# Operands of a float32r matmul and their weights: another place within 128 bytes of SBUF

## The chip, the core and the metric

The kernel runs on one core of a Trainium2 chip. Its engines work side by side and wait for each other through semaphores: TensorE multiplies matrices (PE in the profile; its weight loads are listed apart, as PEld), VectorE (DVE), ScalarE (ACT) and GpSimd (POOL) work on elements, and SyncE (SP) issues the DMAs. On-chip memory, SBUF, has 128 partitions; a tile takes the same bytes of each partition, and "address" means here the byte within a partition. Matmuls write to PSUM.

The metric is the time on the device in microseconds (us), the median over several runs.

## The reference

One layer on 1024 tokens and 16 learned meta tokens, model width 1024, all in float32:

```
h = h + 0.5 * swiglu(rms_norm(h), gate1, up1, down1)      # FFN1, width 2816
proj = rms_norm(h) @ w_in
h = h + concat(stick_breaking_attention(proj), rwkv7_time_mix(proj)) @ w_out
h = h + 0.5 * swiglu(rms_norm(h), gate2, up2, down2)      # FFN2, width 2816
return rms_norm(h)[:, 16:]

swiglu(n, g, u, d) = (silu(n @ g) * (n @ u)) @ d
```

The attention has 8 heads of 64, the recurrence (RWKV-7) 8 heads of 64 with a state of 64 x 64 per head. Nearly all the arithmetic is in the matmuls with the big weight matrices.

## The kernel before

**Float32 in three products.** A float32 operand x is split into a high part `h` (x rounded to the format float32r by ScalarE) and a low part `l` (x minus `h`, by VectorE or GpSimd). A product of two such operands is three matmuls into the same PSUM tile (`mm3`): weights high by operand high, weights high by operand low, weights low by operand high. Weights come by DMA as `wraw` and are split into `whi` and `wlo`. Names that end in `h` and `l` are such pairs: `nh`, `nl` for the normalized input, `ah`, `al` for the activations between the FFN's matmuls.

In a matmul a block of 128 x 128 weights is stationary, and the other operand, 128 rows by up to 512 columns, moves past it. Each matmul has a weight load of its own, which runs beside the matmul before it.

**Two groups of tokens.** Group 0 has the meta tokens and the first 512 tokens (528 columns, `NA`), group 1 the other 512 (`NB`). The order is: FFN1 of group 0, projections of group 0, FFN1 of group 1, projections of group 1, w_out of group 0, FFN2 of group 0, w_out of group 1, FFN2 of group 1 (the "last FFN"); attention and recurrence are woven in between.

**Quads.** In FFN1 of group 0 and in the last FFN, the gate and up matmuls of most pairs of output blocks go another way. The two weight blocks of a pair (a1 and a2), the two halves of the inner dimension and the two halves of the columns form a 2 x 2 by 2 x 2 product, done with seven products in place of eight, as in Strassen's scheme (Winograd's form). `sums` makes the sums of operand halves: tiles `t1` to `t4`, each `h` and `l`, in `Fast.__init__`, of 4 inner blocks by w columns (w = 264 in FFN1, 256 in the last FFN). `pair` makes the sums of weight halves: GpSimd and VectorE write a sum to `qs`, ScalarE and VectorE split it into a pair of tiles `qh`, `ql` of 4 blocks by 128 columns. Two of the seven products use `whi` and `wlo` of a1 itself, the other five a `q` pair. `quad` runs the seven products in the order b11, b21, t1, t2, t4, b22, t3, where b11, b21 and b22 are parts of the normalized input (`n` in FFN1, `n2B` in the last FFN). One product is 4 inner blocks by 3 matmuls:

```
for k in range(4):
    mm(wh[:, k, :], xh[:, k], first and k == 0, False)
    mm(wh[:, k, :], xl[:, k], False, False)
    mm(wl[:, k, :], xh[:, k], False, k == 3)
```

So a pass of `quad` (one gate or up pair) is 7 x 12 = 84 matmuls: 24 with weights from `whi`/`wlo` and 60 with weights from `q`. FFN1 of group 0 has 8 gate and 7 up passes (output blocks 6 to 21, the last up pair goes the plain way), the last FFN 9 gate and 8 up passes (blocks 4 to 21). The order of gates, ups and downs is that of `quad_order`.

**Order of the work.** A planner (`Clock`) runs through the program when it is built: it prices each instruction by its engine and its shape, and issues in the order of its clock. It fixes the order of each engine's queue.

**Where tiles lie.** A pool is a stretch of SBUF in which its tiles stand one after another, each rounded up to 32 bytes. Pools are stacked from the left (from address 16512 up: `const`, `w`, `state`, `ffn`, `hn`, later `stage`) or from the right (from 229344 down). The pools of the quads are stacked from the right, in the order `p`, `t`, `q`; a pool `q` has 2 `wraw` of 4096 bytes, 7 `qh`, 7 `ql`, 3 `qs` and two pairs `ah`, `al`. A tile is written out in full rows, so that block k of a tile of [P, 4, w] begins 4 x w x k bytes after its start. The program before places what this change touches so:

| tile | pool, side | starts at | start modulo 128 | bytes from block to block |
|---|---|---|---|---|
| `ones` | `const`, left | 17024 | 0 | - |
| `whi`, `wlo` | `w`, left | 26816, 35008 and one 4096 on | 64 | 512 |
| `state0`, `state1` | `state`, left | 43200, 43712 | 64 | - |
| `ah`, `al` | `ffn`, left | 48320 and every 2112 on | 64 and 0 by turns | - |
| `nh0`, `nh1`, `nl0`, `nl1` | `hn`, left | 89856 and every 8448 on | 0 | 2112 |
| `t1h` and on, FFN1 | `t`, right | 176544 and every 4224 on | 32 | 1056 |
| `qh`, `ql`, FFN1 | `q`, right | 133280 and every 2048 on | 32 | 512 |
| `n2B` (`h0`, `h1`, `l0`, `l1`) | `f2b`, right | 196576 and every 8192 on | 96 | 2048 |
| `t1h` and on, last FFN | `t`, right | 128992 and every 4096 on | 96 | 1024 |
| `qh`, `ql`, last FFN | `q`, right | 85984 and every 2048 on | 96 | 512 |
| `ah`, `al`, last FFN's quads | `q`, right | 120800 and every 2048 on | 96 | - |
| `vs`, attention of group 0 | `attn0`, right | 179488, 184608 | 32 | 512 |
| `ath`, `atl`, attention of group 0 | `attn0`, right | 212960 and every 2048 on | 96 | - |

"Offset" below is the address at which the moving operand of a matmul starts, less the address at which the weights start that are loaded beside it, modulo 128. A moving operand of 256 columns is 1024 bytes of each partition, a block of weights 512.

Of the kernel before, what the change touches and what calls it, by code (L numbers as in the profile page):

```python
# [7 lines left out]
F32 = mybir.dt.float32  # L8
F32R = mybir.dt.float32r
# [7 lines left out]
P = 128  # L17
# [8 lines left out]
C = 64  # L26
# [13 lines left out]
        dict(raw=1, qs=4, kh=4, vs=2, sg=8, f=2, at=4, z=2, t=2, o=1)]  # L40
WOUT = ((0, 1, 2, 3, 4, 5, 6, 7, 2, 3, 4, 5), (0, 1, 2, 3, 4, 5, 6, 7))
QF = dict(ffn1=6, ffn2=4)
AHEAD = 0.1
IDLE = 0.45
BACKLOG = 3.0
# [14 lines left out]
def quad_order(nm):  # L60

    parts, qf = FPARTS[nm], QF[nm]
    for i, (f0, f1) in enumerate(parts):
# [26 lines left out]
class Eng:  # L90


    def __init__(self, real, name, clk):
        self._r, self._n, self._c = real, name, clk
# [94 lines left out]
class Clock:  # L189
# [195 lines left out]
    def catch_up(self, now):  # L385

        while True:
            best = nxt = None
            for e, l in self.pend.items():
                c, pick = self.clk[e], None  # L390
                for o in l:
                    t = o.at()
                    if t is None:
                        continue
                    key = (max(t, c, self.port if o.port else self.dma - BACKLOG if e == "s" else 0.0)
                           - AHEAD * (o.prio[0] == -self.URGENT), o.prio)
                    if pick is None or key < pick[0]:
# [67 lines left out]
class Fast:  # L465
# [3 lines left out]
    def __init__(self, pools, w):  # L469
        self.p, self.tp, self.q = pools  # L470
        self.w, self.nq, self.nc, self.ns, self.k = w, 7, 7, 4, 0
        self.t = {i: [self.tp.tile([P, 4, w], F32R, name="t%d%s" % (i, c)) for c in "hl"] for i in (1, 2, 3, 4)}


class Ker:
# [99 lines left out]
    def pair(self, raws, out):  # L575


        nc, p = self.nc, self.fast.q
        nb = self.fast.nq
        a1, a2 = raws  # L580
        lo4, hi4 = slice(0, 4), slice(4, 8)

        def part(src=None):

            for tag in ("qh", "ql"):
                yield self.need(bank=(p, tag, nb))
            if src:
                yield self.need(bank=(p, "qs", 3))
            self.clock.ahead = True
            t = [p.tile([P, 4, P], F32R, tag=tag, bufs=nb, name=tag) for tag in ("qh", "ql")]  # L590
            self.hold(t)
            if src:
                x, y, op, eng = src
                raw = p.tile([P, 4, P], F32, tag="qs", bufs=3, name="qs")
                self.hold((raw,))
                eng.tensor_tensor(out=raw, in0=x, in1=y, op=op)
                self.clock.ahead = False
                return t, raw
            return t

        def halves(t, raw):
            self.clock.ahead = True
            self.split(t[0], t[1], raw)
            self.clock.ahead = False
            self.drop((raw,))
            out.append((t, t))
        for tag in ("wh", "wl"):
            yield self.need(bank=(self.wp, tag, 2))
        self.clock.ahead = True
        w = [self.wp.tile([P, KT, P], F32R, tag="w" + c, bufs=2, name=n) for c, n in (("h", "whi"), ("l", "wlo"))]  # L610
        self.hold(w)
        self.clock.ahead = False
        s1 = yield from part((a2[:, lo4], a2[:, hi4], ALU.add, nc.gpsimd))
        self.clock.ahead = True
        self.split(w[0], w[1], a1)
        out.append(([w[0][:, lo4], w[1][:, lo4]], ()))
        out.append(([w[0][:, hi4], w[1][:, hi4]], w))
        self.clock.ahead = False
        s2 = yield from part((s1[1], a1[:, lo4], ALU.subtract, nc.vector))
        halves(*s1)  # L620
        a22 = yield from part()
        self.split(a22[0], a22[1], a2[:, hi4])
        self.clock.ahead = False
        s4 = yield from part((a1[:, hi4], s2[1], ALU.subtract, nc.vector))
        halves(*s2)
        out.append((a22, a22))
        s3 = yield from part((a1[:, lo4], a2[:, lo4], ALU.subtract, nc.gpsimd))
        halves(*s4)
        halves(*s3)
# [71 lines left out]
    def consts(self, cp):  # L701
        nc = self.nc
        self.ident = cp.tile([P, P], F32, name="ident")
        make_identity(self.tc.nc, self.ident)
        self.ones = cp.tile([P, P], F32, name="ones")
        nc.gpsimd.memset(self.ones, 1.0)

    def consts2(self, cp, xp, psp):
# [185 lines left out]
    def ffn(self, nm, h, n, chunks, edge, bank, first=None, hook=None, wx=False, poll=None, resid=None, done=None, wy=False, fast=False, once=False):  # L894
# [125 lines left out]
        act = []  # L1020
        qf, PS = (QF[nm], FPARTS[nm]) if fast else (0, PARTS)
        for part in PS:
# [250 lines left out]
    def plan(self):  # L1273
# [13 lines left out]
        def ffn(nm, poll=False, wx=False, fast=False, once=False):  # L1287
# [3 lines left out]
            def down(f0, f1, q):  # L1291
                dw = self.A[nm + "_w_down"][0].rearrange("(f p) m -> p f m", p=P)
                mw = KT // (f1 - f0) * P
                return dw[:, f0:f1, q * mw:q * mw + mw], f1 - f0, mw
            qf = QF.get(nm, 0)
            for f0, f1 in FPARTS[nm] if fast else PARTS:
# [800 lines left out]
    def pool(self, name, **k):  # L2097
        return Pool(self.tc.alloc_tile_pool(name=name, reuse_waits="tile", **k), self.clock)
# [6 lines left out]
    def body(self):  # L2105
        nc, A = self.nc, self.A
        pool = self.pool
        x, meta = A["x"][0], A["meta_tokens"]
        cp = pool("const", bufs=1)
# [10 lines left out]
        self.xbd = dt("xbd", [P, KT, NB])  # L2120


        self.sp = pool("state", bufs=1)
        self.fp = fp = pool("ffn", bufs=1)
        self.hp = pool("hn", bufs=1)
        h = self.hp.tile([P, KT, NA], F32, name="h")
# [6 lines left out]
        ext = [psp, "g", 4]  # L2133
# [153 lines left out]
        def firstA():  # L2287
            yield from self.ffn("ffn1", h, n, chA, chA, bank, first, hookA, True, None,
                                lambda: F.get("consts"), fast=True)
            ext.clear()  # L2290
            F["first"] = True
            self.carry = {k: self.stp.tile([P, 1], F32, name="car" + k)
                          for k in ["la", "lb"] + [a + str(i) for a in "rkv" for i in range(4)]}


        self.state = [self.sp.tile([P, 2, C], F32, name="state%d" % i) for i in range(2)]
        f2 = {}

        def task(gen, flag):
# [107 lines left out]
        def dense():  # L2407
            ch = [(0, 512)]
            yield from firstA()

            def load_n1(i):
# [85 lines left out]
        ck.spawn(self.loads(self.plan()), 41)  # L2497
        ck.spawn(self.splits(), 40)
        ck.run()
        for p_ in (ext[0], self.psd, f2["p"], fp, self.sp, self.wp, cp, self.dp):  # L2500
            p_.release()


# [28 lines left out]
```

## Time and profile before

| what | us |
|---|---|
| median of 3 runs | 2263.47 (2262.48 to 2263.78) |
| span of the profiled execution | 2259.5 |
| TensorE busy in it | 2232.4 |
| VectorE busy | 1550.5 |
| ScalarE busy | 1098.0 |
| GpSimd busy | 564.3 |
| matmuls, and weight loads | 16409 each |

The span runs from the first to the last instruction of one execution under the profiler. In the profile's rows a group reads: line, engine, operation, output tile <- input tiles, shape, xcount | busy us, mean ns of one | idle time before. All instructions have one line (L104), that of the helper which records them, so groups are told apart by tiles. Durations of matmuls overlap, since they are pipelined: what a matmul costs in a dense stretch is the distance from its start to the start of the next. That distance is read from the timeline, or from the chain of waits, whose merged pieces give the time and the number of matmuls in one stretch.

### The profile page before, as it was taken

How to read it: one execution, taken by the hardware profiler on the slowest of the kernel's cores; microseconds unless marked ns; L12 is line 12 of the kernel's file. 1: busy time of each engine (PE TensorE's matmuls, PEld its weight loads, DVE VectorE, ACT ScalarE, POOL GpSimd, SP SyncE). 2: the span in 40 equal slices, each digit the busy share in tenths (PEclk: the TensorE clock that was granted, in tenths of full speed). 3: DMA queues.
4: the chain of work that ended last, by engine and by line, in shares of the span. 5: the costliest groups of instructions: out<-in, count | busy, mean ns of one | idle time of the engine just before them, and what ended most of it. 6: DMA issues, size and time to landing. Idle time of an engine off the chain costs nothing.

```text
span 2259.5 us, 41724 instructions
## 1 busy us (share of the span) xinstructions
PE 2232.4 (99%) x16409; PEld 1978.1 (88%) x16409; DVE 1550.5 (69%) x2633; ACT 1098.0 (49%) x2176; POOL 564.3 (25%) x722
## 2 busy tenths in 40 slices
PE   9999999999999999999999999999999999999998
PEld 8999999999878888778778987887877899899998
DVE  5887776475666655576576787547777656897774
ACT  6444444534444434555435564445656335454444
POOL 1221111013143231532012324324443001221110
PEclk9999999999999999999999999999999999999999
DMA  5543332545633232332546534333221434333332
GB/s 173 174 113 103 88 100 78 171 132 137 196 111 97 75 101 90 99 91 75 159 141 188 164 106 120 86 100 110 75 85 52 145 112 126 108 97 110 103 91 79
DMA packets 408731, 257.62 MB, mean 114 GB/s; under 512 B 45005, under 2 KB 392357, under 8 KB 408534
## 3 DMA queue, kind: packets, MB, share of 16 engines
q1 hardware_dynamic: 408534, 254.95, 38.4%
q8 instruction: 129, 2.11, 0.4%
q14 instruction: 68, 0.56, 0.1%
HBM read 220.90 MB, written 33.99 MB: 113 GB/s over the span
## 4 chain that ended last, share of the span: by engine, by line
PE 92%; DVE 4%; ACT 1%; issue 1%; DMA 1%; POOL 0%; DVEq 0%; SPq 0%; ACTq 0%
PE pd L104 34%; PE pu L104 21%; PE pg L104 20%; PE pwo L104 3%; PE px L104 3%; PE po L104 2%; PE pz L104 2%; PE pat L104 2%; DVE wlo L104 1%; PE pG L104 1%; DVE tt L104 0%; PE psw L104 0%; ACT whi L104 0%; DVE nl L104 0%; PE pp L104 0%
## 5 line engine op out<-in xcount | busy, mean ns | idle before, releaser
L104 ACT ACTIVATE whi<-wraw 128x1024 fp32r<-128x1024 f32 x314 | 330.6, 1053 | 336.2 <-PE pd L104 213.2
L104 DVE TENSOR_TENSOR wlo<-wraw,whi 128x1024 fp32r<-128x1024 f32 (+1 forms) x312 | 400.7, 1285 | 96.6 <-ACT whi L104 90.8
L104 PE MATMUL pd<-ah,whi 128*128 128x512 f32 (+2 forms) x944 | 326.2, 346 | 2.8 <-DVE h L104 1.9
L104 PE MATMUL pd<-ah,wlo 128*128 128x512 f32 (+2 forms) x944 | 319.6, 339 | 1.2 <-DVE wlo L104 1.2
L104 PE MATMUL pd<-al,whi 128*128 128x512 f32 (+2 forms) x944 | 319.1, 338 | 0.4 <-DVE al L104 0.2
L104 PE MATMUL pd<-nh,whi 128*128 128x256 f32 (+7 forms) x648 | 211.0, 326 | 0.0
L104 PE MATMUL pu<-nh,whi 128*128 128x512 f32 (+3 forms) x576 | 206.6, 359 | 0.0
L104 PE MATMUL pd<-nl,whi 128*128 128x256 f32 (+7 forms) x648 | 205.5, 317 | 0.0
L104 PE MATMUL pd<-nh,wlo 128*128 128x256 f32 (+7 forms) x648 | 205.1, 317 | 0.0
L104 PEld LDWEIGHTS pd<-ah,whi 128*128 128x128 f32 x944 | 177.8, 188 | 25.6 <-DVE h L104 3.2
L104 PE MATMUL pg<-nh,whi 128*128 128x512 f32 (+3 forms) x536 | 197.7, 369 | 1.6 <-DVE h L104 0.8
L104 PE MATMUL pu<-nl,whi 128*128 128x512 f32 (+3 forms) x576 | 198.1, 344 | 0.0
L104 PE MATMUL pu<-nh,wlo 128*128 128x512 f32 (+3 forms) x576 | 198.0, 344 | 0.0
L104 PEld LDWEIGHTS pd<-ah,wlo 128*128 128x128 f32 x944 | 177.9, 188 | 22.3 <-DVE wlo L104 2.1
L104 PEld LDWEIGHTS pd<-al,whi 128*128 128x128 f32 x944 | 178.0, 189 | 18.5 <-DVE al L104 1.5
L104 POOL TENSOR_TENSOR qs<-wraw 128x512 f32<-128x512 f32 x64 | 97.3, 1524 | 374.3 <-DVE ql L104 124.5
L104 PE MATMUL pg<-nl,whi 128*128 128x512 f32 (+3 forms) x536 | 188.7, 352 | 0.9 <-DVE nl L104 0.9
L104 PE MATMUL pg<-nh,wlo 128*128 128x512 f32 (+3 forms) x536 | 188.4, 352 | 0.0
L104 DVE SCALAR_TENSOR_TENSOR h<-pd,h 128x256 f32<-128x256 f32 (+1 forms) x200 | 107.6, 541 | 75.8 <-PE pd L104 74.8
L104 POOL TENSOR_TENSOR al<-sl,ah 128x512 fp32r<-128x512 f32 (+2 forms) x45 | 72.5, 1612 | 316.7 <-ACT ah L104 307.1
L104 PEld LDWEIGHTS pd<-nh,whi 128*128 128x128 f32 (+2 forms) x648 | 121.0, 187 | 12.3 <-issue 3.1
L104 PEld LDWEIGHTS pd<-nh,wlo 128*128 128x128 f32 (+2 forms) x648 | 121.0, 187 | 8.5
(395 smaller groups left out, 5650.1 us busy)
## 6 DMA issues: line engine op xcount, KB each, us to landing
wraw<-in_ffn_w_gate_dram SPq DMA_DIRECT2D x90, 512.0 KB
wraw<-in_ffn_w_up_dram SPq DMA_DIRECT2D x90, 512.0 KB
wraw<-in_ffn_w_down_dram SPq DMA_DIRECT2D x88, 512.0 KB
wraw<-in_w_in_dram SPq DMA_DIRECT2D x54, 512.0 KB
wraw<-in_w_out_dram SPq DMA_DIRECT2D x20, 512.0 KB
s<-rkvd SPq DMA_DIRECT2D x18, 256.0 KB
raw<-qkvd SPq DMA_DIRECT2D x16, 264.0 KB
raw<-qkvd SPq DMA_DIRECT2D x16, 256.0 KB
```

The costliest lines, as they stand in the source:

```text
L104: self._c.trace(self._n, op, lambda: f(*a, **k), out, [x for x in args if isinstance(x, bass.AP)], k)
```

## The change

The tiles `qh` and `ql` are declared as 4 x 136 elements (`QROW`) in place of 4 x 128. Of these, 4 rows of `qrow` elements are used as before, 128 of each: `qrow` is 128 + w % 128, so 136 in FFN1 (w = 264) and 128 in the last FFN (w = 256). `qs` is 16 elements longer, `ones` 24. The recurrence's two `state` tiles (1024 bytes together) come from the pool `stage` in place of a pool of their own, which goes; `stage` opens after FFN1's quads. No instruction is added or removed.

```
+QROW = P + 8
...
+        self.qrow = P + w % P
         self.t = {i: [self.tp.tile([P, 4, w], F32R, name="t%d%s" % (i, c)) for c in "hl"] for i in (1, 2, 3, 4)}
...
-        nb = self.fast.nq
+        nb, qrow = self.fast.nq, self.fast.qrow
...
-            t = [p.tile([P, 4, P], F32R, tag=tag, bufs=nb, name=tag) for tag in ("qh", "ql")]
+            t = [p.tile([P, 4 * QROW], F32R, tag=tag, bufs=nb, name=tag) for tag in ("qh", "ql")]
+            t = [x[:, 0:4 * qrow].rearrange("p (k m) -> p k m", m=qrow)[:, :, 0:P] for x in t]
...
-                raw = p.tile([P, 4, P], F32, tag="qs", bufs=3, name="qs")
+                raw = p.tile([P, 4 * P + 16], F32, tag="qs", bufs=3, name="qs")[:, 0:4 * P].rearrange("p (k m) -> p k m", m=P)
...
-        self.ones = cp.tile([P, P], F32, name="ones")
+        self.ones = cp.tile([P, P + 24], F32, name="ones")[:, 0:P]
...
-        self.sp = pool("state", bufs=1)
...
+            self.state = [self.stp.tile([P, 2, C], F32, name="state%d" % i) for i in range(2)]
             self.carry = {k: self.stp.tile([P, 1], F32, name="car" + k)
...
-        self.state = [self.sp.tile([P, 2, C], F32, name="state%d" % i) for i in range(2)]
...
-        for p_ in (ext[0], self.psd, f2["p"], fp, self.sp, self.wp, cp, self.dp):
+        for p_ in (ext[0], self.psd, f2["p"], fp, self.wp, cp, self.dp):
```

## The prediction

> **What bounds the kernel now.** I read the page's busy shares first, then the chain of work that ended last.
>
> ```profile
> PE 2232.4 (99%) x16409; PEld 1978.1 (88%) x16409; DVE 1550.5 (69%) x2633; ACT 1098.0 (49%) x2176; POOL 564.3 (25%) x722
> ...
> PE 92%; DVE 4%; ACT 1%; issue 1%; DMA 1%; POOL 0%; DVEq 0%; SPq 0%; ACTq 0%
> ```
>
> TensorE is the bound nearly everywhere: its matmuls cover 99% of the span and 92% of the chain. So the question is at what interval matmuls follow each other in the stretches that the change touches. The windows over the quads of FFN1 and over the last FFN come next (columns: stretch, its length, busy time and count of each engine, clock, DMA share, GB/s).
>
> ```profile
> 135.00:360.00 225.00, 225.00 (x1857) 225.00 (x1856) 174.69 (x268) 108.87 (x190) 43.61 (x28) 1.00 0.34 97
> 1880.00:2240.00 360.00, 358.84 (x2499) 333.58 (x2498) 273.20 (x421) 178.64 (x320) 66.09 (x49) 1.00 0.35 102
> ```
>
> The order is PE, PEld, DVE, ACT, POOL. PE has no gap in 225 us of FFN1's quads and 1.2 us of gaps in 360 us of the last FFN. VectorE, which prepares the weights, is at 174.69/225 = 78% and 273.20/360 = 76%: there is room before it would hold PE up. The granted clock is 1.00, so the clock explains nothing here.
>
> The chain cut to these stretches gives the price of one quad pass (84 matmuls). First FFN1, then, behind it, the last FFN:
>
> ```profile
> 135.08 10.16 PE pg L104 x84
> 145.25 10.17 PE pu L104 x84
> ```
>
> ```profile
> 2034.54 10.00 PE pg L104 x84
> 2044.54 5.58 PE pd L104 x24
> 2050.12 10.00 PE pu L104 x84
> ```
>
> So a step (start to start) is 10.165/84 = 121.0 ns at 264 columns and 10.00/84 = 119.0 ns on average at 256; the 24 matmuls of 512 columns between them take 5.58/24 = 232.5 ns each. The timeline of the last of these passes shows that the 119.0 is a mean of two kinds:
>
> ```profile
> 2051.24 0.28 PE L104 MATMUL pu<-n2Bh,wlo 128*128 128x256 f32 x1
> ...
> 2052.64 0.28 PE L104 MATMUL pu<-n2Bh,wlo 128*128 128x256 f32 x1
> 2052.76 0.28 PE L104 MATMUL pu<-t1h,qh 128*128 128x256 f32 x1
> ...
> 2054.20 0.28 PE L104 MATMUL pu<-t2h,qh 128*128 128x256 f32 x1
> ```
>
> With weights from `whi`/`wlo`, 12 steps take 2052.64 - 2051.24 = 1.40 us, 116.7 ns each; with weights from `qh`/`ql`, 12 steps take 2054.20 - 2052.76 = 1.44 us, 120.0 ns. Columns, clock and stage are the same. As a test, 24 x 116.7 + 60 x 120.0 = 10.0 us, the whole pass. The groups of this stretch say it again, for the matmul and for the weight load that runs beside it:
>
> ```profile
> L104 PE MATMUL pg<-n2Bh,whi 128*128 128x256 f32 x72 | 20.1, 279 | 0.0
> L104 PE MATMUL pg<-t2h,qh 128*128 128x256 f32 x36 | 10.2, 283 | 0.0
> ```
>
> ```profile
> L104 PEld LDWEIGHTS pg<-n2Bh,whi 128*128 128x128 f32 x72 | 13.6, 188 | 0.2
> L104 PEld LDWEIGHTS pg<-t4h,qh 128*128 128x128 f32 x36 | 6.9, 192 | 0.0
> ```
>
> (A duration is the step plus some 163 ns of pipeline.) What differs is where operands lie. By the byte addresses listed under the kernel, `t` and `q` of the last FFN are both at 96 modulo 128: an offset of 0. `n2B` is at 96 and `whi`/`wlo` at 64: an offset of 32. My reading is that the load of the next weights and the moving operand, both read from SBUF at once, get in each other's way when they start in the same 64 bytes of each 128.
>
> **The change part by part.** Offsets after it, from the tile sizes. `ones` grows by 96 bytes, so every pool stacked from the left moves up by 96; without the 1024 bytes of `state`, `ffn` and `hn` move by 96 - 1024, again 96 modulo 128. The pools stacked from the right stay, save `q`: 14 tiles grow by 128 bytes and three `qs` by 64, 1984 in all, so `q` starts 1984 bytes lower, 64 modulo 128.
>
> - A, last FFN, five of seven products of a pass (weights in `q`): 96 - (96 - 64) = 64. From offset 0 to 64.
> - B, `n2B` against `whi`/`wlo`: 96 - (64 + 96) = 64 modulo 128. From 32 to 64, in the quads, at the edges and in w_out's second half.
> - C, FFN1, `t` against `q`: now the blocks k of a product have offsets 0, 32, 64, 96 (1056 bytes a block against 512). Afterwards a block of `q` takes 544 bytes: 64 for every k, but 64 - 544 = 32 modulo 128 where the next load belongs to the next k, one step in three.
> - D, FFN1, `n` against `q`: from 0 and 64 by turns to 32, 64, 96, 0. `n` against `whi`/`wlo` in the dense stages keeps its offsets, both sides having moved alike.
>
> Steps. A is 17 passes (9 gate, 8 up) of 5 x 12 = 60, so 1020. B is 17 x 24 = 408 in the passes, 3 x 128 = 384 of w_out and about 200 at the edges, some 1000. C is 15 passes (8 gate, 7 up) of 4 x 12 = 48, so 720.
>
> The price of a constant offset of 64 isn't in the quads. Three rows bound it. Attention's first group has it in one run (`vs` at 32, `ath`/`atl` at 96, 256 columns):
>
> ```profile
> 979.61 0.28 PE L104 MATMUL po<-atl,vs 128*128 128x256 f32 x1
> 979.73 0.28 PE L104 MATMUL po<-ath,vs 128*128 128x256 f32 x1
> ...
> 980.18 0.28 PE L104 MATMUL po<-ath,vs 128*128 128x256 f32 x1
> 980.30 0.28 PE L104 MATMUL po<-atl,vs 128*128 128x256 f32 x1
> ```
>
> Six steps take 0.69 us, 115 ns; the four in the middle 0.45 us, 112.5 to 114 ns. Second, FFN1's third block, at offset 64, beside its neighbours:
>
> ```profile
> 140.74 0.28 PE L104 MATMUL pg<-t4h,qh 128*128 128x264 f32 x1
> ...
> 141.11 0.29 PE L104 MATMUL pg<-t4h,qh 128*128 128x264 f32 x1
> ...
> 141.47 0.28 PE L104 MATMUL pg<-t4h,qh 128*128 128x264 f32 x1
> ...
> 141.82 0.28 PE L104 MATMUL pg<-t4h,qh 128*128 128x264 f32 x1
> ...
> 142.19 0.29 PE L104 MATMUL pg<-nh,qh 128*128 128x264 f32 x1
> ```
>
> Blocks k = 0 to 3 take 0.37, 0.36, 0.35 and 0.37 us: 123, 120, 117, 123 ns a step. Eight columns are worth 8 x (232.5 - 116.7)/256 = 3.6 ns, so 117 is 113.4 at 256. Third and against it, `n` by `whi`/`wlo`, where offsets 0 and 64 alternate by k:
>
> ```profile
> L104 PE MATMUL pu<-nl,whi 128*128 128x256 f32 x144 | 40.4, 281 | 0.0
> ```
>
> 281 less 163 is 118 ns, and if 0 costs 120 there, 64 costs 116; if nothing is gained by turns, 118. So a constant 64 lies between 113.4 and 118.2 ns. I take 115, from the attention run, the only unbroken one.
>
> Sum: A 1020 x (119.9 - 115) = 5.0 us. B 1000 x (116.7 - 115) = 1.7 us. C: two steps in three at 115 + 3.6 = 118.6, one at 116.7 + 3.6 = 120.3, mean 119.2 against 121.0; 720 x 1.8 = 1.3 us. D mixes the four offsets as C does now: 0. Together 8.0 us.
>
> Matmuls of 512 columns get nothing: the load is hidden behind twice the columns, and a step is 232.5 ns with `ah` at either offset. `state` in another pool moves no instruction; it is first written long after the quads' tiles that shared its new place, in rwkv:
>
> ```profile
> L104 DVE TENSOR_TENSOR state<-px,d x16: 282/289/295, 591.3 to 1493.5; 64x128 f32<-64x128 f32 x16
> ```
>
> It costs 0. The planner prices an operation by its shape, and no shape changes, so the order of the work stays. The split of `q` now writes four runs 544 bytes apart in FFN1; it lies behind the 22% of VectorE's time that is free.
>
> The profiled execution has a span of 2259.5 us; the median of the runs is 2263.5, 4.0 more, which I carry over: 2259.5 - 8.0 + 4.0 = **2255.5 us**.
>
> The Trainium skill speaks against the change: "SBUF — State Buffer", section "Who interferes with whom", gives TensorE two independent read ports, one for the moving operand and one for weight loads, and says that it never waits on anyone. By that the offset does nothing and the time stays at 2263.5. The trace doesn't agree: 120.0 against 116.7 ns, and 192 against 188 ns for the load, in one pass.
>
> **The rivals.**
>
> *The floor.* If 64 ends all collisions, a step is 113.4 ns: A 6.6, B 3.3, C (two in three at 117) 720 x 2.9 = 2.1; 12.0 us, 2251.5. For it: the 113 ns runs are the lowest steps of both widths.
>
> *Little gained.* If a steady 64 costs the 118.2 of the alternating rows, A wins 1020 x 1.7 = 1.7, B loses 1000 x 1.5 = 1.5, C wins nothing: 2263.3. Two streams held at one offset may also lock into some other collision. For it: those rows show no gain of their own, only a mean.
>
> *Nothing.* If loads and moving operands don't meet at all, and the 3 ns come from something else in `q` (its seven buffers, or the products it serves), moving `q` changes nothing: 2263.5. Against it: FFN1's block k = 2 is fast with the same `q`. This is what the section of "SBUF — State Buffer" in the Trainium skill would give.
>
> *Slower.* Only the place within 64 bytes counts, so that 64 is the same as 0. Then A stays, and B goes from its good 32 to the bad place: 1000 x 3.3 = 3.3 us, and the edges of the last down projection some 130 x 3.3 = 0.4, with C up to 720 x 1 = 0.7: 2267.9. It decides from a step of 118.3 ns upward, where A's gain equals B's loss. Against it: 117 ns in FFN1's block k = 2 beside 123 in k = 0.
>
> A supply that falls behind ends there too. VectorE's subtraction into `ql` would have to rise from 731 ns by 50 us / 74 = 0.68 us (the free time of 135 to 360 us over its 74 instructions on `ql`):
>
> ```profile
> 135.00:360.00 225.00, 85.12 (x300) 56.43 (x300) 59.45 (x74) 1.00 0.34 97
> ```
>
> ```profile
> L104 DVE TENSOR_TENSOR ql<-qs,qh 128x512 fp32r<-128x512 f32 x68 | 48.2, 731 | 0.3 <-ACT qh L104 0.3
> ```
>
> Nothing suggests that.
>
> **How the numbers follow.** Forecast 0.42 (2253 to 2259), floor 0.20 (2250 to 2253), little gained 0.20 (2259 to 2265), nothing 0.08 (2262 to 2265), slower 0.10 (2266 to 2270). About 0.2%, 4.5 us, is what a measurement of this kernel tells from no change: 2259.0 and 2268.0. Faster is forecast and floor, 0.62; slower by more is half of the slower case, 0.05; the rest, 0.33, is no change. The range of 2250.5 to 2264.5 leaves out the slower case and the ends of the others. The 3 ns steps are small, so the size is less sure than the sign.
>
> **What would show it.** In the profile after, quad passes of the last FFN fall from 10.00 to 84 x 115 = 9.66 us (9.53 at the floor, 9.93 if little is gained, 10.07 if 64 is 0), and those of FFN1 from 10.17 to (36 x 121.0 + 48 x 119.2)/1000 = 10.08. The load with `qh` falls from 192 to 188 ns; w_out's matmuls on `n2B` fall below 279; those of 512 columns stay at 232.5 ns. A wait of `pg` or `pu` on `ql` longer than the 0.8 us of before would show that the supply fell behind. The prediction is wrong if `t` by `q` still takes 283 ns, or if 512 columns or the dense stages change too.

## The result, and the profile after

| | before | after |
|---|---|---|
| median of 5 runs each, us | 2263.47 (2262.48 to 2265.2) | 2256.35 (2254.84 to 2258.75) |
| ratio after/before, 95% interval | | 0.9968 [0.9956, 0.998] |
| span of the profiled execution, us | 2259.5 | 2257.0 |

The change wins 7.1 us of 2263.47, 0.32%; 2255.5 had been predicted. The profiled execution of after is the slowest of its five (its span and 1.75 us are the 2258.75 of the table), so the two spans differ by less than the medians. A second profile of the same kernel, taken with the last experiments, has a span of 2255.1.

First the busy shares on the page of the kernel after, then its windows over FFN1's quads and the last FFN, with the columns of before:

```profile
PE 2227.9 (99%) x16409; PEld 1972.8 (87%) x16409; DVE 1550.8 (69%) x2633; ACT 1097.6 (49%) x2176; POOL 561.7 (25%) x722
```

```profile
135.00:360.00 225.00, 225.00 (x1854) 225.00 (x1854) 174.77 (x267) 108.89 (x190) 43.62 (x29) 1.00 0.34 97
1880.00:2240.00 360.00, 358.61 (x2540) 332.50 (x2539) 277.09 (x430) 182.73 (x329) 66.52 (x50) 1.00 0.35 103
```

The counts answer before any duration does. In 360 us of the last FFN 2540 matmuls start in place of 2499, 1.6% more; in FFN1's quads it is 1854 in place of 1857, no gain. The chain of waits of the kernel after, cut to FFN1's quads and behind it to the last FFN (start, us, group, number of matmuls), says the same by the pass:

```profile
135.99 10.16 PE pg L105 x84
146.16 10.20 PE pu L105 x84
```

```profile
1966.55 9.53 PE pg L105 x84
1976.08 9.53 PE pu L105 x84
...
2026.78 9.68 PE pu L105 x84
2036.46 9.52 PE pg L105 x84
2045.98 5.58 PE pd L105 x24
2051.57 9.65 PE pu L105 x84
```

A pass of the last FFN fell from 10.00 us to 9.52 or 9.53 in some places and to between 9.64 and 9.80 in others; 9.53/84 is 113.4 ns a matmul. FFN1's passes stay where they were, and 24 matmuls of 512 columns still take 5.58 us. The groups of the last FFN, matmuls and then weight loads:

```profile
L105 PE MATMUL pg<-n2Bh,whi 128*128 128x256 f32 x104 | 29.1, 280 | 0.0
L105 PE MATMUL pg<-t2h,qh 128*128 128x256 f32 x36 | 10.0, 276 | 0.0
```

```profile
L105 PEld LDWEIGHTS pg<-n2Bh,whi 128*128 128x128 f32 x120 | 22.6, 188 | 0.9
L105 PEld LDWEIGHTS pg<-t4h,qh 128*128 128x128 f32 x36 | 6.8, 188 | 0.0
```

Matmuls with weights in `q` went from 283 to 276 ns, their loads from 192 to 188. Those on `n2B` stay at about 280. The one place where the chain shows that `n2B` lost is w_out of group 1, whose 378 matmuls run without a break; first the kernel before, then the second profile of the kernel after:

```profile
1798.62 44.10 PE pwo L104 x378
```

```profile
1800.73 44.52 PE pwo L105 x378
```

116.7 ns a step became 117.8. The supply kept up: the only wait for `ql` in the list of PE's waits is about as long as the 0.8 us of before.

```profile
PE pg L105 <- DVE ql L105: 0.9, 1, 0.9
```

**Where the time came from.** The order of TensorE's 16409 matmuls is the same before and after, so the two traces can be laid over each other. The table sums the distances from start to start by group, waits left out. Mean steps that stand below without a row are worked out in the same way from that kernel's trace.

| group | steps | before, us | after, us | ns a step, before and after |
|---|---|---|---|---|
| last FFN, weights in `q` (A) | 1018 | 122.05 | 115.87 | 119.9, 113.8 |
| last FFN, `n2B` by `whi`/`wlo` (B) | 739 | 86.54 | 85.90 | 117.1, 116.2 |
| w_out, `n2B` by `whi`/`wlo` (B) | 383 | 44.69 | 45.09 | 116.7, 117.7 |
| FFN1, `t` by `q` (C) | 720 | 87.26 | 87.21 | 121.2, 121.1 |
| all of 512 columns | 3607 | 837.0 | 836.9 | 232.0, 232.0 |

A gives 6.2 us, B 0.2, C nothing: 6.4 of the 7.1. The rest is no more than executions of one kernel differ by. Two stretches where the overlaid traces drift apart by 1 to 3 us (the start, and 1300 to 1400 us) lie outside the change: in the second the granted clock of that one execution of after was 0.97, as the window shows, and later profiles of both kernels' variants show 0.97 to 0.99 about there too.

```profile
1300.00:1402.00 102.00, 96.04 (x973) 85.05 (x973) 83.71 (x165) 55.73 (x124) 39.15 (x58) 0.97 0.42 115
```

So the sign and the total were right, but the total was put together wrongly: one term larger, two terms near zero. The experiments ask three things. Is it the offset at all, and does each matmul follow its own? Why did B gain next to nothing, although its offset is the same 64? Why did FFN1 gain nothing?

### The profile page after: what moved, and what is told of

It is laid out like the page before. It is cut to its first block, busy times and chain, and to the rows that moved or that the text cites. A ratio compares the mean times of both kernels' runs of the same rounds, so it can differ in the third digit from the quotient of the medians.

```text
span 2257.0 us, 41723 instructions
## 1 busy us (share of the span) xinstructions
PE 2227.9 (99%) x16409; PEld 1972.8 (87%) x16409; DVE 1550.8 (69%) x2633; ACT 1097.6 (49%) x2176; POOL 561.7 (25%) x722
## 4 chain that ended last, share of the span: by engine, by line
PE 92%; DVE 4%; ACT 1%; DMA 1%; issue 1%; POOL 0%; SPq 0%; DVEq 0%; ACTq 0%; POOLq 0%
PE pd L105 35%; PE pu L105 21%; PE pg L105 20%; PE pwo L105 4%; PE px L105 3%; PE po L105 2%; PE pz L105 2%; PE pat L105 2%; DVE wlo L105 1%; PE pG L105 1%; DVE tt L105 0%; PE psw L105 0%; ACT whi L105 0%; PE pp L105 0%; PE pss L105 0%
```

## The experiments

Edits are against the kernel after unless said otherwise. All rows are of the chain of waits, except where another view is named. The kernel before was measured again beside every set of runs, with medians from 2263.02 to 2264.23 us, and each ratio is to it; times of different sets differ by that much without any cause in the kernel.

**q0: A alone undone.** `q` of the last FFN back at offset 0, its tiles as wide as after the change.

```
-raw = p.tile([P, 4 * P + 16], F32, tag="qs", bufs=3, name="qs")[:, 0:4 * P].rearrange("p (k m) -> p k m", m=P)
+raw = p.tile([P, 4 * P + (0 if self.fast.w == 256 else 16)], F32, tag="qs", bufs=3, name="qs")[:, 0:4 * P].rearrange("p (k m) -> p k m", m=P)
```

> The changed kernel, but the three qs tiles of the last FFN are 64 bytes shorter each, so that its q tiles come to lie 64 bytes off and meet t and n2B at offset 0 again; the 2176 bytes from one q tile to the next, FFN1, the shift of whi/wlo and the place of state stay. Theory (the offset alone sets the step): the 60 steps of a pass on q go back from 113.8 to 120 ns, a pass from 9.6 to about 9.95 us, and the time rises by 1020 x 6.2 ns = 6.3 us, from 2256.4 to 2262.6. Rival (the spacing of the q tiles, the place of state or the shift of the left side earned it): passes stay at 9.6 us and the time at 2256.4.

Measured: 2263.88 us (12 runs), ratio to before 0.9995 [0.9986, 1.0003]. Passes of the last FFN:

```profile
2010.35 9.87 PE pg L105 x84
2020.22 5.60 PE pd L105 x24
2025.83 9.99 PE pu L105 x84
```

Steps of `q` take 119.1 ns, while w_out stays at 117.7 and the rest as after. The 64 bytes of padding of each of the three `qs` buffers, which no instruction reads, carry nearly the whole gain: it is where `q` lies, neither the tiles' width nor `state`. One thing does not fit a price set by the offset modulo 128 alone: in the kernel before, nearly all steps of `q` at offset 0 took 119 to 121 ns, and here they spread from 112 to 131. The `q` tiles are 2176 bytes apart here and were 2048 apart; no run shows whether that is the reason.

**w32: B alone undone.** `ones` of 128 columns, so that `n2B` by `whi`/`wlo` is at 32 again.

```
-self.ones = cp.tile([P, P + 24], F32, name="ones")[:, 0:P]
+self.ones = cp.tile([P, P], F32, name="ones")[:, 0:P]
```

> The changed kernel with ones of 128 columns as before, so that whi/wlo meet n2B at offset 32 again, while q stays at 64. Theory (each step follows its own offset): the matmuls on q keep 113.8 ns; those of n2B by whi/wlo go to 116.7 ns everywhere: w_out's 384 fall from 117.7, 0.4 us less, the 408 of the quads rise from 115.4, 0.5 us more; time 2256.4, within 1 us. Rival (a run of steps keeps the pace with which it begins, and q's fast steps need fast ones on whi ahead of them): passes rise to 9.8 us or more, and the time by 3 us or more.

Measured: 2258.63 us (6 runs), ratio 0.9972 [0.9961, 0.9983]. Passes of the last FFN, with `q` at 64 and `n2B` at 32:

```profile
2024.85 9.68 PE pu L105 x84
2034.52 9.60 PE pg L105 x84
```

Steps with `q` take 113.9 ns and those with `whi`/`wlo` 116.7 everywhere: 24 x 116.7 + 60 x 113.4 = 9.60, the second row. Here each matmul follows its own offset, and B's part of the change is worth nothing that the time can show.

**c0: C alone undone.** FFN1's `qh`, `ql` and `qs` as before the change.

```
-self.qrow = P + w % P
+self.qrow = P
...
-t = [p.tile([P, 4 * QROW], F32R, tag=tag, bufs=nb, name=tag) for tag in ("qh", "ql")]
+t = [p.tile([P, 4 * (QROW if self.fast.w == 256 else P)], F32R, tag=tag, bufs=nb, name=tag) for tag in ("qh", "ql")]
...
```

> The changed kernel with FFN1's q tiles placed as before (rows of 128 elements, no spare bytes in qs: offsets 0, 32, 64, 96 by k); the last FFN and whi/wlo as changed. Theory (the change to FFN1 does nothing, since one step in three stays at 32 there): FFN1's passes 10.17 us as before against 10.19 changed, time 2256.4 less 0.3. Rival (it brought a part of the gain that the rows hide): time 2258 or more.

Measured: 2257.95 us (5 runs), ratio 0.9967 [0.9955, 0.9978]. FFN1's passes:

```profile
135.26 10.16 PE pg L105 x84
145.42 10.23 PE pu L105 x84
```

The time, 0.05 us below the rival's 2258, does not decide; the passes do, and they didn't change: C is worth nothing, though single blocks of `t` differ (117.4 ns at offset 64, 122 to 124 at the others).

**t64: all of `t` by `q` in FFN1 at 64.** The first guess was that one step in three at offset 32 spoils the others. Blocks of `t` 1152 bytes apart and of `q` 512 leave none; there are three `sn` buffers in place of four, to make room.

```
-self.t = {i: [self.tp.tile([P, 4, w], F32R, name="t%d%s" % (i, c)) for c in "hl"] for i in (1, 2, 3, 4)}
+self.t = {i: [self.tp.tile([P, 4, w + w // 264 * 24], F32R, name="t%d%s" % (i, c))[:, :, 0:w] for c in "hl"] for i in (1, 2, 3, 4)}
...
```

> The changed kernel with t's blocks in FFN1 at 1152 bytes, nine times 128, from each other (24 spare columns), q's blocks at 512 and one buffer sn fewer, which makes room: the offset of t and q is 64 in every step of FFN1, also where the next load belongs to the next block. Theory (the one step in three at 32 spoils FFN1's gain): 48 of a pass's 84 steps fall from 121.2 to 117 ns, a pass from 10.19 to 9.99 us, the time by 15 x 0.20 = 3.0 us to 2253.4. Rival (264 columns, 1056 bytes, are no multiple of 128 and can't hold the good pace): passes stay at 10.2 us, time 2256.4.

Measured: 2258.42 us (6 runs), ratio 0.9971 [0.996, 0.9982]. FFN1's passes:

```profile
136.33 10.19 PE pg L105 x84
146.51 10.23 PE pu L105 x84
```

The guess fell. A constant 64 at 264 columns goes at 121.0 to 121.4 ns, 3.6 ns for the eight columns above the 117.7 that w_out has at 64. Both failures thus look alike: a constant offset of 64 seems to have, beside the 113.4, a slower pace of 117.7; below they are called the early and the late pace. In the kernel after, w_out's run was at 117.7 without a break, and behind four small matmuls (`nps`, one column each) at 1847 us its last four steps were at 113.4.

**kick: the late run broken.** One added matmul (`warm`, 128 columns, into a bank that nobody reads) ahead of each of w_out's eight blocks.

```
+            if late and i == 0:
+                yield self.need(bank=self.nextbank)
+                self.warm(self.bank("warm"))
             yield self.need(*[x[k][:, cs] for k in range(KT) for x in n[0:2]], bank=self.nextbank)
             pd = self.bank("pwo")[:, 0:256]
```

> One more matmul (the one that warms the clock, into a PSUM bank that nobody reads) ahead of every block of output of w_out of group 1, so that its run of some 380 matmuls on n2B by whi/wlo at offset 64 is broken eight times. After the change all of these had 117.7 ns a step but the last four after a pause, which had 113.4. Theory (two paces, and what comes ahead of a run decides which one it takes): at least one of the eight blocks goes at 113.4 ns, 48 steps in 5.45 us against 5.65, and the blocks differ from each other. Rival (w_out's n2B by whi/wlo costs 117.7 by itself, by its own offset or by the engines beside it): all blocks stay at 117.7. The added matmuls cost 1 to 3 us, so the whole time, 2257 to 2260, decides nothing.

Measured: 2256.93 us (one run). The first blocks:

```profile
1800.91 0.22 PE warm L105 x2
1801.13 5.47 PE pwo L105 x48
1806.60 0.22 PE warm L105 x2
1806.82 5.47 PE pwo L105 x48
```

All eight blocks went over to the early pace, not only one. The timeline shows the change of pace within four steps:

```profile
1800.89 0.37 PE L105 MATMUL pwo<-n2Bh,whi 128*128 128x256 f32 x1
1801.09 0.28 PE L105 MATMUL pwo<-n2Bl,whi 128*128 128x256 f32 x1
1801.21 0.28 PE L105 MATMUL pwo<-n2Bh,wlo 128*128 128x256 f32 x1
1801.33 0.28 PE L105 MATMUL pwo<-n2Bh,whi 128*128 128x256 f32 x1
...
1801.67 0.28 PE L105 MATMUL pwo<-n2Bh,whi 128*128 128x256 f32 x1
```

0.20 us for the step behind `warm`, two of 0.12, and then 0.34 us for each three, 113.4 ns a step. Operands, their addresses and the order of the matmuls are the same; only what stands ahead differs. (The added matmul may also shift which PSUM bank a block writes to; n64, below, takes the early pace without that.) A break costs what it brings: 0.22 + 5.47 = 5.69 us against 48 x 117.7 = 5.65. A single one ahead of the first block was not run.

**bkick: the same break at offset 32.** The same edit in the kernel before.

> The kernel before the change, with the same matmul as in the run 'kick' ahead of each block of w_out of group 1, where n2B by whi/wlo is at offset 32. Theory (only offset 64 has an early pace that is held; a break does nothing at other offsets): the blocks stay at 116.7 ns a step, wandering between about 113 and 120. Rival (a break quickens any run of matmuls, whatever its offset, so that the gain in w_out was the break's and not the offset's): the blocks go at 113.4 ns here too.

Measured: 2265.68 us (one run).

```profile
1801.57 0.22 PE warm L104 x2
1801.79 5.61 PE pwo L104 x48
1807.40 0.22 PE warm L104 x2
1807.62 5.66 PE pwo L104 x48
```

No early pace: the blocks take 116.9 and then 117.9 ns a step, against 116.7 before, and single steps wander between 112 and 121. The break helps at 64 and not at 32; at offsets 0 and 96 it wasn't tried.

**q32_w96 and q96_w0: the other offsets.** `q` of the last FFN at 32 and 96, `n2B` by `whi`/`wlo` at 96 and 0.

```
-raw = p.tile([P, 4 * P + 16], F32, tag="qs", bufs=3, name="qs")[:, 0:4 * P].rearrange("p (k m) -> p k m", m=P)
+raw = p.tile([P, 4 * P + (24 if self.fast.w == 256 else 16)], F32, tag="qs", bufs=3, name="qs")[:, 0:4 * P].rearrange("p (k m) -> p k m", m=P)
-self.ones = cp.tile([P, P + 24], F32, name="ones")[:, 0:P]
+self.ones = cp.tile([P, P + 16], F32, name="ones")[:, 0:P]
```

These are the lines of q32_w96; q96_w0 has 8 in place of 24 and 8 in place of 16.

> In the last FFN the weights in q are placed for an offset of 32 (t by q), and ones has 16 elements more in place of 24, which gives n2B by whi/wlo an offset of 96. Theory (the offset modulo 128 sets the step, whichever tiles are involved): t by q goes to the 116.7 ns that n2B by whi/wlo had at 32 before. Offset 96 hasn't been measured alone: if only the distance from 0 counts, 96 is as 32, 116.7 ns; if what counts is which of the two is ahead, it differs from 32, between 113.4 and 120. Whole time: the kernel after plus 1020 x 2.8 ns = 2.9 us, about 2259. Rival (what made q quick was only its place, any place other than 0): t by q stays at 113.8 ns, 2256.

> In the last FFN the weights in q are placed for an offset of 96 (t by q), and ones has 8 elements more in place of 24, which gives n2B by whi/wlo an offset of 0. Theory (the offset modulo 128 sets the step, whichever tiles are involved): n2B by whi/wlo takes the 120.0 ns that t by q had at 0 before; t by q has the same step as n2B by whi/wlo at 96 in the run with 32 and 96 exchanged. Whole time: 1000 x 2.9 ns for n2B and 1020 x 2.8 ns for q, 5.8 us above the kernel after, about 2262. Rival (w_out and the products of whi/wlo have a step of their own near 117): n2B stays at 116.7 to 117.7 ns.

Measured: 2262.9 and 2267.52 us (one run each). w_out, first in q32_w96 (offset 96), then in q96_w0 (offset 0):

```profile
1800.31 44.73 PE pwo L105 x378
```

```profile
1803.12 45.35 PE pwo L105 x378
```

Offset 0 costs `n2B` 45.35/378 = 120.0 ns, just what it cost `q` before, on other tiles. 96 costs 118.3 here and 119.1 in `q`, and 32 costs `q` 118.1, not the 116.7 expected from `n2B`. So at 32 and 96 there is no fixed price; steps wander, and how they average depends on the run. Both expected times were too low for that (2259 and 2262). Offset 0 held 120.0 in the kernel before and here, though not in q0; only at 64 was a run seen to keep to 113.4.

**n64: `n` at a constant 64 in the dense stages.** Rows of `nh`, `nl` 2176 bytes apart in place of 2112; FFN1's `q` as in c0.

```
-half = [[self.hp.tile([P, 4, NA], F32R, tag="n%s%d" % (c, q), name="n%s%d" % (c, q)) for q in range(2)] for c in "hl"]
+half = [[self.hp.tile([P, 4, NA + 16], F32R, tag="n%s%d" % (c, q), name="n%s%d" % (c, q))[:, :, 0:NA] for q in range(2)] for c in "hl"]
...
```

> The tiles nh and nl of group 0 get rows of 544 columns in place of 528 (2176 bytes from block to block in place of 2112), so that n by whi/wlo has an offset of 64 for every k in the dense stages of group 0, where 0 and 64 alternated; FFN1's q is as in the kernel before. Theory A (each matmul's step follows its own offset, and a constant 64 gives the quick pace of 113.4 ns at 256 columns): the 256-column rows of n by whi/wlo fall from 281 ns to 276 ns and the whole falls by up to 2800 x 4.3 ns = 12 us below the kernel after, to about 2246. Theory B (a constant 64 is held at one of two paces, and stretches entered from matmuls of 512 or of 264 columns take the late one, 117.7 ns): nothing changes beyond 1 us, 2256 to 2258, rows stay at 281. Matmuls of 512 columns stay at 232.5 ns by both.

Measured: 2253.08 us (5 runs), ratio 0.9955 [0.9941, 0.9969]. Neither theory was right. Of the matmuls of 256 columns with `n` by `whi`/`wlo`, those that move `nl` fell from 118.2 to 117.1 ns a step and those that move `nh` stayed at 118.0: close to theory B, and a constant 64 did not give them the early pace. Where the time was won is told with its repeat, below.

**f64k: everything in FFN1 at 64, and a break ahead of each pass.** n64 and t64 together, with a `warm` matmul into each pass's own bank ahead of its first product.

```
         px = yield from new("x")
+        if w == 264:
+            self.warm(px)
         yield from product(px, x["b11"], True)
```

> In FFN1 of group 0 every product of a quad but one now has a constant offset of 64: blocks of t 1152 bytes apart and of q 512, rows of n 2176 bytes apart (b22, n by q, is at 96), with two sn buffers in place of four; and one matmul that warms the clock goes ahead of each of the 15 passes, which breaks the run as the one ahead of w_out's blocks did. Theory A (264 columns have the two paces too, and FFN1 stays at the late one, 121.3 ns, because its matmuls follow each other without a break): behind the break b11, b21, t1, t2 and t4, 60 steps, go at 117.0 ns, so that a pass takes 9.9 us or less in place of 10.2, its added matmul included (0.2 us). Theory B (264 columns have no early pace that is held: 1056 bytes of the moving operand are no multiple of 128, so that each step starts at another phase): the steps stay at 121, and a pass takes 10.4 us. Whole time by A 2254 to 2256, by B 2257 to 2260.

Measured: 2257.62 us (one run). FFN1's passes with their two added steps:

```profile
135.31 10.47 PE pg L105 x86
145.78 10.45 PE pu L105 x86
```

Theory B held: 10.45 less 0.22 is 10.23, no faster than without. Behind each break the steps soon go 119, 122, 121, 122, 121 and on around 121.2. No run shows 264 columns at an early pace that is held. That 1056 bytes are no multiple of 128, as 1024 are, might explain it, but no run here shows why.

**after2 and n64b: both kernels again, on one chip.**

> The kernel after the change once more, side by side with the run that has n's rows of 544 columns too. Theory (the pace of a run is set by the program's order and addresses, not by chance of an execution): w_out's blocks of group 1 on n2B again go at 117.7 ns, all but the last four steps, and the last FFN's passes behind the first down projection at 9.52 to 9.80 us; 2256 to 2258 us. If the pace is drawn anew in each execution, the blocks are at 113.4 or mixed in this profile.

> The kernel with n's rows of 544 columns again, beside the kernel after, to see whether it is the faster of the two. Theory (one pace per program): w_out's blocks at 113.4 ns again, 1.6 us less than the kernel after; its first run was 3.3 us below the kernel after, measured at another time, so 2253 to 2255 us and a ratio below the kernel after's. If the pace is drawn anew, no difference that lasts: 2256.

Measured: after2 2257.07 us (7 runs), ratio to before 0.9972 [0.996, 0.9983]; n64b 2252.43 us (5 runs), ratio 0.995 [0.9937, 0.9962]. The medians differ by 4.6 us in favour of n64b, after 3.3 the first time; the two intervals overlap by 0.0002 at their ends, while the slowest run of n64b, 2256.09, is below the fastest of after2, 2256.21. Both kept w_out at its pace of the first time. w_out and a block of 512 columns in n64b, and the same block in after2:

```profile
1796.62 42.84 PE pwo L105 x378
...
822.01 5.52 PE pg L105 x24
827.53 5.52 PE pu L105 x24
```

```profile
823.19 5.56 PE pg L105 x24
828.75 5.56 PE pu L105 x24
```

w_out goes at 42.84/378 = 113.3 ns without any added matmul, in n64, n64b and f64k alike; in the kernel after, q0, c0 and t64 it goes at 117.7, each time. Its own addresses are the same in all of them. What differs is where `n` lies, in the stretch of 512 columns just ahead of it. So the pace is not drawn by chance: a program kept it in both of its profiles, and what runs ahead sets it. What that does is not as simple as kick makes it look. Near the end of w_out the four `nps` matmuls break the run in every kernel. First after2, then n64b, from the timeline:

```profile
1845.09 0.50 PE L105 MATMUL nps<-ones,nacc 128*128 128x1 f32 x4
...
1845.77 0.28 PE L105 MATMUL pwo<-n2Bh,wlo 128*128 128x256 f32 x1
...
1846.22 0.40 PE L105 MATMUL pg<-nh,whi 128*128 128x512 f32 x1
```

```profile
1839.31 0.50 PE L105 MATMUL nps<-ones,nacc 128*128 128x1 f32 x4
...
1839.99 0.28 PE L105 MATMUL pwo<-n2Bh,wlo 128*128 128x256 f32 x1
...
1840.46 0.39 PE L105 MATMUL pg<-nh,whi 128*128 128x512 f32 x1
```

The last four steps of w_out take 0.45 us in after2, the early pace behind a late run, and 0.47 us in n64b, the late pace behind an early run. After, q0, c0 and t64 do as after2; kick, n64 and f64k as n64b. A break thus lets a run change its pace either way. The last FFN of after2 says the same: the six passes that follow another pass begin with 24 steps at 113.3 to 113.4 ns, but of the eleven that follow matmuls of 512 columns seven begin at 117.6 to 117.9 and four at 113.8. Which property of the stretch ahead decides, no run here shows.

The second gain was not expected. Laid over each other, the matmuls of 512 columns that move `nl` take 233.3 ns in after2 and 228.8 in n64b, 823 of them: 3.7 us. Those that move `nh` stay at 231.3. The group of the gates' matmuls from 600 to 1000 us shows it as well, 396 ns in after2 and then 391 in n64b:

```profile
L105 PE MATMUL pg<-nl,whi 128*128 128x512 f32 x142 | 56.2, 396 | 0.0
```

```profile
L105 PE MATMUL pg<-nl,whi 128*128 128x512 f32 x141 | 55.2, 391 | 0.0
```

With 1.7 us from w_out and 1.7 from the 256 and 272 columns of group 0 that makes 7.1 us; 1.1 of it is lost again in other steps and waits, for the overlaid traces end 6.0 us apart (spans 2255.1 and 2249.1). It is the fastest kernel that was run, below the one before by 0.5% and below the one after by some 0.2%.

## Why the prediction was right, and where it was not

- **The reading of the cause** was right in that the offset sets the step. Weights that start in the same place of 128 bytes as the operand moving beside them cost 120.0 ns a step on two kinds of tiles (`q` before, `n2B` in q96_w0), and q0 takes nearly the whole gain back with one offset. The rivals "nothing" and "slower" are out: 64 is better than 0 at 256 columns. The condition given for it, a start "in the same 64 bytes of each 128", was wrong: `n2B` at 96 and `whi` at 64 lie in the same half and cost 116.7 ns (the kernel before), `n2B` at 96 and `whi` at 0 lie in different halves and cost 118.3 (q32_w96). That the two reads get in each other's way fits the loads, 192 ns at offset 0 and 188 at 64, but no run shows it directly. The Trainium skill, "SBUF — State Buffer", section "Who interferes with whom", calls TensorE's port for the moving operand and the one for weight loads independent and says that TensorE never waits on anyone. These traces don't agree: the same products take 120.0 ns a step at offset 0 and 113.4 at 64.
- **A** had its mechanism right and was too small: 5.0 us against 6.2, since the steps went to 113.8 ns, close to the floor of 113.4, and not to 115.
- **B** is the step that failed. "So a constant 64 lies between 113.4 and 118.2 ns. I take 115" gave one price to what has two. w_out took the late pace, 117.7, and lost 0.4 us; in the last FFN it was mixed (114.4 for the gates' matmuls on `n2B`, 116.2 for the ups', within the passes) and won 0.6. Together 0.2 in place of 1.7 us. The bounds were the two paces; a value between them was not one that a run was seen to hold. The rivals "the floor" (113.4) and "little gained" (118.2) had priced one each. The six steps of attention from which 115 came were the early pace in their middle with longer steps at the edges, and six steps could not show that a run may also stay at another pace.
- **C** failed too: 0 in place of 1.3 us. The 117 ns of FFN1's block k = 2 was read as a price of offset 64 that more blocks would get. t64 and f64k gave it to nearly all, and they went at 121: what a block does between blocks at other offsets is not what it does in a run of its own kind.
- **D** was taken as 0 and cost 0.2 us: the 180 steps of `n` by `q` in FFN1 went from 120.5 to 121.8 ns. **`state`** cost nothing that shows.
- **512 columns:** they kept their 232.5 ns, but the reason given, that the load is hidden behind twice the columns, does not hold for all of them: in n64 those that move `nl` win 4.5 ns where all offsets are 64.
- **The sum** was 8.0 us and the steps gave 6.4. That the time came out within 0.9 us of the forecast is partly luck: A's excess of 1.2 us paid for less than half of the 2.8 that B and C lacked.

The Trainium skill, "TensorE: Matmul & The Clock Gate", section "Wait — 56ns, not 53.3ns?", gives a warm matmul N ÷ 2.4 GHz and about 2.5 ns. By that 256 columns would take 109.2 ns, an estimate from that section's figures. The trace differs: the early pace is 113.4, so even here 6.7 ns lie above N ÷ 2.4, and the measured paces decide.

## What to carry to other kernels

Where matmuls of some 256 columns follow each other without a gap, print for each product the address of the moving operand less that of the weights loaded beside it, modulo 128: here a constant 64 gave up to 5.5% over a constant 0 for a few bytes of padding. Then look at the steps and not at the offset alone, since a run can settle at a late pace, and what comes ahead of it decides. Try a constant 64 in every dense stage before rearranging any work (the rows of `n` brought another 0.2% here), and take a price for the forecast from a long steady run of the same shape, not from a handful of steps.

## What the runs showed of the hardware that was not expected

- At offset 64 and 256 columns TensorE holds one of two paces, 113.4 or 117.7 ns a step, for up to 378 matmuls. What runs ahead decides which: one added matmul moved whole blocks from the late one to the early one (kick), other rows of `n` in the stretch ahead did the same (n64), and the four `nps` matmuls move w_out either way. A program took the same pace in w_out in both of its profiles.
- At offset 0 nearly all steps took 119 to 121 ns in `q` of the kernel before and in w_out of q96_w0, but in q0 they spread from 112 to 131 with a mean of 119.1. At 32 and 96 steps wander between 112 and 134 ns, with means from 116.7 to 119.1.
- 264 columns stay near 121 ns at a constant 64, with a break or without; 117 shows only in single blocks between others.
- The offset reaches matmuls of 512 columns as well, though only every third: 233.3 to 228.8 ns for those that move `nl`.
